# Four smallest experts last, summed in one tile, and a final layernorm that starts beside them

## The chip, the cores and the metric

The kernel runs on one core of a Trainium2 chip. The metric is the device time of one execution in microseconds (us); lower is better. A core has TensorE (PE, matrix products into PSUM), VectorE (DVE), ScalarE (ACT), GpSimd (POOL) and SyncE (SP, which here only issues transfers). Each engine works through its own instructions in program order and waits on semaphores of the others. Sixteen DMA engines serve the transfers that SyncE and GpSimd ask for.

## The reference, cut to what matters

One decoder layer over 1024 tokens of width 1024, all in float32: a token mixer, a first layernorm, and a mixture of 32 experts (512 hidden units), with a second layernorm at the end. The change touches only the mixture and the last layernorm.

```python
h2 = x * (1 + sc2) + sh2                       # the router and the experts read this
# top-1 of 4 groups, then top-2 of that group's 8 experts: 2 experts for each token
gu = h2[tokens_of_e] @ w_up[e]                 # 1024 x 1024
m[tokens_of_e] += weight * ((silu(gu[:, :512]) * gu[:, 512:]) @ w_down[e])   # 512 x 1024
x = _layernorm(ALPHA * x + (1 + g2) * m, ln2_g, ln2_b)       # over the 1024 columns
```

How many tokens an expert gets depends on the data; the mean is 64.

## The kernel before, in words

The mixer, the first layernorm and the routing take the first half of the time and aren't touched. They leave in DRAM `h2d` (the experts' inputs), `xad` (ALPHA times x, one row for each token, plus 128 spare rows for the padding of the lists) and `wd` (the weights of the tokens), and in SBUF the lists `tokp` and `aidp` (tokens of each expert) and `nhp` (a size code for each expert: over 9 means more than 32 tokens, over 11 more than 64, over 15 more than 128).

**Experts.** 32 experts are computed one after the other. The first four positions hold fixed experts; the other 28 are ordered by size (`places`, `reorder`): `place` gives the rank that stands at each position, so that large and small ones alternate. Positions 25 to 31 hold the ranks 28, 7, 29, 11, 30, 15, 31, where rank 31 is the smallest. Rank 7, at position 26, may have two blocks of 128 tokens.

**Weights.** Each expert has six tiles of 1 MB (four of w_up, two of w_down). SyncE asks for them in the order of `SEQ`: up(e), then down(e - 1). They go into 19 tiles of SBUF that are used in turn: `release` gives a tile back after its matmuls and asks for the next one (`eload`). After the last weights `late_v` reads the two layernorm vectors ln2_g and ln2_b into the two halves of a tile (`l2`), each repeated over 128 partitions.

**One step.** The step of expert e is: up(e) on the first two tiles, turn the hidden values of expert e - 1 (`turn_hidden`: four TensorE transposes, a ScalarE copy into `eh`), up(e) on the last two tiles, `hidden(e)` (Silu on ScalarE, product on VectorE), turn the tokens of e + 1, and `last_of(e - 1)`: `down`, then `finish`. GpSimd gathers the token rows and the weights ahead (`gather_first`, `gather_weight`). By `by_parts` a matmul takes the whole width for more than 64 tokens (`up_whole`, `down_whole`), and 64 or 32 columns of TensorE for fewer (`up_parts`, `down_parts`). `finish` multiplies the result by the weights on VectorE into `eyo` and adds it to the rows of `xad` by an accumulating indirect transfer from GpSimd (`scatter`). Each of these waits for the one before.

**Last layernorm.** After the experts all engines read a flag: if some expert has more blocks than were computed, a general loop does the rest (not taken with these inputs). Then SyncE reads the 1024 rows of `xad` as eight tiles `rt[0]` to `rt[7]` of 128 x 1024. `t_ops` gives the operations of a tile: mean and variance by VectorE (V in `TSTAT`) or by two ScalarE passes (S), a square root, and scaling and shifting divided among VectorE, GpSimd and ScalarE by `TMODE`. `TORDER` is the written-out order in which the operations of the eight tiles are issued. Each tile is then stored to `out`.

All instructions stand in program order on their engines (`manual_schedule`); nothing is moved by a scheduler.

Of the kernel before, what the change touches and what calls it, by code (L numbers as in the profile page):

```python
# [9 lines left out]
F32 = mybir.dt.float32  # L10
# [41 lines left out]
TSTAT = "VVVSVSVS"  # L52
TMODE = "pFBpFAFF"
TORDER = "00100102101213023231320425323423564546436567545653776777575"
# [5 lines left out]
def tile_hybrid_moe_layer(  # L60
# [786 lines left out]
    for j, (base, step) in enumerate(((16, 4), (FIXED, 1), (17, 4), (8, 1), (18, 4), (12, 1), (19, 4))):  # L847
        G.iota(spread[:, :, j], pattern=[[step, 4]], base=base, channel_multiplier=0, **imp)

# [442 lines left out]

    nmax = cst([P, 1], I32, "nmax")
    places()
# [94 lines left out]
    def down(e, ks, w):  # L1389
        p = pd(e)  # L1390

        def whole():
            down_whole(p, eh, ks, w)
            if e in TWO:
                with tc.If(N[e] > 15):
                    down_whole(pup2, eh2, ks, w)

        by_parts(N[e], whole, lambda m: down_parts(m, p, eh, ks, w))
# [87 lines left out]
    def last_of(e):  # L1486
        down(e, range(8, 12), weights_of(e, range(8, 12)))
        release(e, range(8, 12))
        finish(e)
        finish_second(e)  # L1490

    for e in range(NE):
        up(e, range(4), weights_of(e, range(4)))
# [30 lines left out]
    most = count(nmax, 0, None, 1)  # L1524
    with tc.If(most > 0):
# [30 lines left out]

    l2g, l2b = l2
    rt = [h for _ in range(4) for h in halves(unused.popleft())]
    for tt in range(8):
        nc.sync.dma_start(rt[tt], xad[tt * P:(tt + 1) * P, :])  # L1560
    st8 = p4.tile([P, 8, 2, 6], F32, name="st8")
    mv8 = p4.tile([P, 8, 2], F32, name="mv8")

    def t_ops(tt):
        r, mode = rt[tt], TMODE[tt]
        mu, sd = mv8[:, tt, 0:1], mv8[:, tt, 1:2]

        def moments():
            for n, sl in enumerate(COLS):
                V.bn_stats(st8[:, tt, n], r[:, sl])  # L1570

        def root(scale=1.0):
            S.activation(sd, sd, AF.Sqrt, bias=eps, scale=scale)

        def shift():
            if TSTAT[tt] == "V":
                V.scalar_tensor_tensor(mu, mu, -1.0, sd, op0=OP.mult, op1=OP.mult)
            else:
                V.tensor_tensor(mu, mu, sd, op=OP.mult)

        def part(q, sl, fused, e):
            v = (l2g, l2b)[q]
            if not fused:
                e.tensor_tensor(r[:, sl], r[:, sl], v[:, sl], op=(OP.mult, OP.add)[q])
            elif q:
                V.scalar_tensor_tensor(r[:, sl], r[:, sl], sd, v[:, sl], op0=OP.mult, op1=OP.add)
            else:
                V.scalar_tensor_tensor(r[:, sl], r[:, sl], mu, v[:, sl],
                                       op0=OP.subtract if TSTAT[tt] == "V" else OP.add, op1=OP.mult)

        def both(q):
            e = {"p": (G, G), "F": (V, V), "A": (G, V), "B": (V, G), "X": (V, V), "q": (G, G)}[mode][q]
            for sl in COLS if tt == 7 else [slice(0, D)]:
                part(q, sl, mode == "F", e)
                if q and tt == 7:
                    nc.sync.dma_start(out[0, tt * P:(tt + 1) * P, sl], r[:, sl])
            if q and tt < 7:
                nc.sync.dma_start(out[0, tt * P:(tt + 1) * P, :], r)

        if TSTAT[tt] == "V":  # L1600
            ops = [moments, lambda: V.bn_aggr(mv8[:, tt], st8[:, tt]), root]
        else:
            ops = [lambda: S.activation(eyo[0], r, AF.Copy, accum_out=mu),
                   lambda: V.tensor_scalar(mu, mu, -1.0 / D, None, op0=OP.mult),
                   lambda: S.activation(eyo[0], r, AF.Square, bias=mu, accum_out=sd),
                   lambda: root(1.0 / D)]
        ops.append(lambda: V.reciprocal(sd, sd))
        if mode == "q":
            ops.append(lambda: V.tensor_scalar(r, r, mu, sd, op0=OP.subtract if TSTAT[tt] == "V" else OP.add,
                                               op1=OP.mult))  # L1610
        elif mode != "F":
            ops += [shift, lambda: S.activation(r, r, AF.Identity, bias=mu, scale=sd)]
        return ops + [lambda: both(0), lambda: both(1)]

    t_all = [t_ops(tt) for tt in range(8)]
    for tt in TORDER:
        run(t_all[int(tt)], 1)
# [23 lines left out]
```

## Time and profile before

| | us |
|---|---|
| median of 3 runs (lowest to highest) | 1169.26 (1168.99 to 1174.07) |
| the profiled execution, its own time | 1171.18 |
| its span | 1169.3 |
| TensorE busy in the span | 1038.5 (89%) |
| VectorE busy | 553.8 (47%) |
| ScalarE busy | 292.7 (25%) |
| GpSimd busy | 358.9 (31%) |

The span is the stretch from the first to the last instruction that the profiler saw; times below are us from its start. The granted clock is the share of its full 2.4 GHz at which TensorE ran; it has two levels, 1.00 (2.4 GHz) and 0.50 (1.2 GHz), and a mean of a stretch can lie between. DMA share is the mean busy share of the sixteen DMA engines. Over the whole span 304.50 MB were moved.

### The profile page before, as it was taken

Reading aid. Unit: us, or ns where it says so; the run is one execution under the profiler, and the core shown is the slowest. Engines: PE = TensorE matmul, PEld = TensorE weight load, DVE = VectorE, ACT = ScalarE, POOL = GpSimd, SP = SyncE. Lnnn points to the kernel's source line nnn. Section 1 sums busy time; section 2 is a strip of 40 time slices with the busy share of each in tenths; the row PEclk is TensorE's granted clock in tenths of the full one; section 3 lists DMA queues with packets and bytes.
Section 4 is the critical chain, followed back from the end, with each engine's and each line's share of the span. In section 5 each row is a group of like instructions: output and inputs, shape, how many; then the busy total and the mean of one; then the engine's idle time right before and its main releaser. Section 6 shows DMA issues by size and latency. Waiting matters only on the chain.

```text
span 1169.3 us, 16712 instructions
## 1 busy us (share of the span) xinstructions
PE 1038.5 (89%) x5758; PEld 687.5 (59%) x5758; DVE 553.8 (47%) x1018; ACT 292.7 (25%) x440; POOL 358.9 (31%) x271
## 2 busy tenths in 40 slices
PE   4999999899999989998678999899999999899920
PEld 3778888788788767777433454454444544454510
DVE  6858975737664489999511211130223113211338
ACT  3363326643224442221210110010011101110113
POOL 2325543262211236543412211231134113301225
PEclk9899999999999999999798999999999999899975
DMA  9954454444212325414999989999999999999964
GB/s 277 247 168 145 131 182 140 142 144 144 91 51 59 144 88 221 164 68 187 371 361 345 393 338 323 381 394 412 386 377 380 412 389 373 390 416 394 387 222 179
DMA packets 93631, 304.50 MB, mean 260 GB/s; under 512 B 14769, under 2 KB 42073, under 8 KB 68909
## 3 DMA queue, kind: packets, MB, share of 16 engines
q1 hardware_dynamic: 83900, 275.52, 63.4%
q0 software_dynamic: 8368, 22.90, 7.3%
q10 hardware_dynamic: 1216, 4.21, 0.9%
q8 instruction: 83, 1.36, 0.5%
q14 instruction: 64, 0.52, 0.1%
HBM read 281.09 MB, written 22.88 MB: 260 GB/s over the span
## 4 chain that ended last, share of the span: by engine, by line
PE 27%; DMA 25%; issue 25%; DVE 16%; ACT 3%; POOLq 1%; POOL 1%; SPq 1%; DVEq 0%; ACTq 0%
DMA xad<-yo,tokp 19%; DMA wr<-wd,aidp 4%; PE sm L302 4%; PE acc L623 3%; PE acc L625 3%; PE acc L624 3%; PE acc L621 2%; PE acc L619 2%; PE acc L620 2%; DVE y1a L234 1%; DMA wd<-w 1%; DVE pc L1022 1%; DVE Fg L886 1%; DMA xad<-Vv 1%; SPq L103 1%
## 5 line engine op out<-in xcount | busy, mean ns | idle before, releaser
L1406 DVE TENSOR_TENSOR act<-up,act 128x512 f32<-128x512 f32 x32 | 22.1, 692 | 299.7 <-ACT act L1405 244.3
L1427 POOL DMA_INDIRECT xad<-yo,tokp x36 | 52.9, 1470 | 231.7 <-DVE yo L1423 106.1
L1423 DVE SCALAR_TENSOR_TENSOR yo<-dn,wr,g2p 32x256 f32<-32x256 f32 (+2 forms) x94 | 52.1, 563 | 126.9 <-PE ov L1359 39.0
L1412 ACT ACTIVATE eh<-tp 128x512 f32<-128x512 f32 x36 | 21.1, 596 | 315.5 <-PE tp L1411 274.8
L623 PE MATMUL acc<-whi,hTh 128*128 128x512 f32 x192 | 83.1, 433 | 0.0
L1212 POOL DMA_INDIRECT KS<-h2d,tokp x32 | 30.6, 958 | 164.0 <-PE tp L1319 155.1
L166 ACT ACTIVATE whi<-wr 128x1024 fp32r<-128x1024 f32 (+1 forms) x44 | 44.9, 1021 | 128.1 <-PE acc L625 67.9
L625 PE MATMUL acc<-whi,hTl 128*128 128x512 f32 x192 | 76.0, 396 | 0.0
L624 PE MATMUL acc<-wlo,hTh 128*128 128x512 f32 x192 | 75.4, 393 | 0.0
L167 POOL TENSOR_TENSOR wlo<-wr,whi 128x1024 fp32r<-128x1024 f32 (+1 forms) x15 | 35.8, 2385 | 119.9 <-ACT whi L166 108.3
L302 PEld LDWEIGHTS sm<-QP,KS 128*128 128x128 f32 x448 | 58.2, 192 | 7.3 <-issue 3.3
L619 PE MATMUL acc<-hTh,whi 128*128 128x512 f32 x144 | 59.3, 411 | 0.0
L302 PE MATMUL sm<-QP,KS 128*128 128x64 f32 x448 | 56.1, 269 | 2.6 <-DVE KS L315 1.6
L1344 PE MATMUL up<-pring,ext 128*128 128x512 f32 x128 | 56.7, 593 | 1.6 <-DVE yo L1423 1.6
L621 PE MATMUL acc<-hTh,wlo 128*128 128x512 f32 x144 | 56.9, 395 | 0.5 <-DVE wlo L167 0.3
L881 PE MATMUL pa<-wh,yl 128*128 128x512 f32 (+1 forms) x128 | 51.8, 405 | 5.5 <-DVE yl L865 5.5
L620 PE MATMUL acc<-hTl,whi 128*128 128x512 f32 x144 | 56.7, 393 | 0.0
L880 PE MATMUL pa<-wl,yh 128*128 128x512 f32 (+1 forms) x128 | 51.3, 401 | 4.7 <-DVE wl L1052 4.7
L879 PE MATMUL pa<-wh,yh 128*128 128x512 f32 (+1 forms) x128 | 53.4, 417 | 1.5 <-ACT wh L1051 0.9
L1405 ACT ACTIVATE act<-up 128x512 f32<-128x512 f32 x32 | 19.1, 597 | 135.2 <-PE ov L1344 52.3
L443 POOL TENSOR_TENSOR vec<-vec,y1a 128x1024 f32<-128x1024 f32 x14 | 35.4, 2527 | 55.2 <-ACT y1a L442 55.2
L167 DVE TENSOR_TENSOR wlo<-wr,whi 128x1024 fp32r<-128x1024 f32 (+1 forms) x29 | 38.4, 1324 | 22.6 <-ACT whi L166 21.9
(476 smaller groups left out, 2243.2 us busy)
## 6 DMA issues: line engine op xcount, KB each, us to landing
pring<-in_w_up SPq DMA_DIRECT2D x52, 1024.0 KB, 20.5
pring<-in_w_down SPq DMA_DIRECT2D x28, 1024.0 KB, 8.5
ring<-in_w_up SPq DMA_DIRECT2D x28, 1024.0 KB, 16.4
wr<-in_w_in SPq DMA_DIRECT2D x44, 512.0 KB, 6.0
y1a<-in_w_ada SPq DMA_DIRECT2D x32, 512.0 KB, 4.0
ring<-in_w_down SPq DMA_DIRECT2D x12, 1024.0 KB, 20.4
y0a<-in_w_up SPq DMA_DIRECT2D x8, 1024.0 KB, 15.1
y0b<-in_w_up SPq DMA_DIRECT2D x8, 1024.0 KB, 24.3
```

The source lines that it names most:

```text
L167: (G if u % 3 == 2 and u > W8 else V).tensor_tensor(lo, w, hi, op=OP.subtract)
L302: PE.matmul(p[:, hd], chd(KS)[:, c4, hd], chd(QP)[:, c4, hd].rearrange("p (b two i) -> p b two i", two=2, i=h)[:, :, 1, :], start=True, st ...
L619: PE.matmul(a[i], hi[:, j, sl], hTh[k], start=st, stop=False)
L620: PE.matmul(a[i], hi[:, j, sl], hTl[k], start=False, stop=False)
L621: PE.matmul(a[i], lo[:, j, sl], hTh[k], start=False, stop=sp)
L623: PE.matmul(a[i], hTh[k][:, sl], hi[:, j], start=st, stop=False)
L624: PE.matmul(a[i], hTh[k][:, sl], lo[:, j], start=False, stop=False)
L625: PE.matmul(a[i], hTl[k][:, sl], hi[:, j], start=False, stop=sp)
L879: PE.matmul(p, yh[:, k], wh[k][:, sl], start=k == 0, stop=False)
L1344: PE.matmul(p[:, h], x[:, k], gate_up(w[k], 2, h), start=k == 0, stop=k == 7)
L1423: V.scalar_tensor_tensor(yo[rows, n * c:(n + 1) * c], src, w[rows], g2p[rows, n * c:(n + 1) * c], op0=OP.mult, op1=OP.mult)
L1427: G.indirect_dma_start(out=xad, out_offset=bass.IndirectOffsetOnAxis(ap=tcol[rows], axis=0), in_=yo[rows], in_offset=None, bounds_check=T ...
```

## The change

- **Order of experts.** Positions 25 and 27 now hold the ranks 15 and 11, and positions 28 to 31 the ranks 28 to 31: the four smallest come last.
- **Their results.** If none of the four has more than 32 tokens and no general loop is needed (flag `slow` is 0), their results aren't scattered: `finish` writes each into 32 rows of one tile `yo2`. One 128 x 128 matrix `same_` (1 where two rows belong to the same token) sums the rows of one token on TensorE (`late_sum`). The rows of `xad` of these tokens are gathered into `base`, the sum is added, the result normalized (`late_stats`, `late_norm`) and written over the plain result by an indirect store (`late_store`).
- **All rows.** At the end of step 29, after the last weights and the two vectors have been asked for, SyncE asks for all eight tiles of `xad` (`late_start`); they hold everything but the last four experts.
- **Normalization.** Its operations are issued in eight groups, `norms(0)` to `norms(7)`, some within steps 31 and after it. GpSimd has no share in them. Tiles 0, 2 and 4 (P) are scaled and shifted on TensorE by a diagonal matrix and a product of ones with ln2_b, and taken out of PSUM by ScalarE; the others take two VectorE passes. Statistics are VectorE's for tiles 0 and 3 and ScalarE's for the others.
- **The last expert's** hidden values are turned into `eh2`, as `eh` takes the diagonals.
- If `slow` isn't 0, the four are scattered as before, the rows are read again and normalized after that.

```diff
-TSTAT = "VVVSVSVS"
-TMODE = "pFBpFAFF"
-TORDER = "00100102101213023231320425323423564546436567545653776777575"
+TSTAT = "VSSVSSSS"
+TMODE = "PFPFPFFF"
+TORDER = "001012001X02132X2451106X71X022X22XX23435647334535464654574576664777".split("X")
+LATE0 = 28
...
+    for o, n, base in ((25, 1, 15), (27, 1, 11), (LATE0, 4, LATE0)):
+        G.iota(place[:, o:o + n], pattern=[[1, n]], base=base, channel_multiplier=0, **imp)
...
+        V.tensor_reduce(slowi, nhp[:, LATE0:NE], axis=AX.X, op=OP.max)
+        V.tensor_scalar(slowi, slowi, 9.0, None, op0=OP.is_gt)
+        V.tensor_tensor(slowi, slowi, nmax, op=OP.max)
+        for i in range(4):
+            V.tensor_copy(tokl[32 * i:32 * (i + 1)], tokp[0:32, 0, LATE0 + i:LATE0 + i + 1])
+        V.tensor_copy(tokf, tokl)
...
     def finish(e):
+        if e < LATE0:
+            finish_any(e)
+            return
+        r = 32 * (e - LATE0)
+        with tc.If(slow[0] > 0) as large:
+            finish_any(e)
+        with large.Else():
+            for q in range(4):
+                sl = slice(q * 256, (q + 1) * 256)
+                V.scalar_tensor_tensor(yo2[r:r + 32, sl], pd(e)[32 * q:32 * (q + 1), 0, 0:256], wr[e % 2][0:32],
+                                       g2p[0:32, sl], op0=OP.mult, op1=OP.mult)
+
+    slow = []
+
+    def finish_any(e):
         yo = eyo[e % 2]
...
-    def last_of(e):
-        down(e, range(8, 12), weights_of(e, range(8, 12)))
+    def last_of(e, between=lambda: None, h=eh):
+        down(e, range(8, 12), weights_of(e, range(8, 12)), h)
         release(e, range(8, 12))
+        between()
         finish(e)
         finish_second(e)
...
+    base = xg[2]
...
+    def late_loads():
+        for tt in range(8):
+            nc.sync.dma_start(rt[tt], xad[tt * P:(tt + 1) * P, :])
+
+    def late_start():
+        rt.extend(h for _ in range(4) for h in halves(unused.popleft()))
+        late_loads()
+        G.indirect_dma_start(out=base, out_offset=None, in_=xad,
+                             in_offset=bass.IndirectOffsetOnAxis(ap=tokl, axis=0), bounds_check=T + P - 1,
+                             oob_is_err=False)
+        V.tensor_scalar(act2[:, 0:P], ones, tokf, None, op0=OP.mult)
+        p = tp()
+        PE.matmul(p[:, 0], act2[:, 0:P], ident, start=True, stop=True)
+        V.tensor_scalar(same_, p[:, 0], tokf, None, op0=OP.is_equal)
+
+    def late_sum():
+        for n in range(2):
+            PE.matmul(pup2[:, n], same_, yo2[:, COLS[n]], start=True, stop=True)
+
+    mu8, sd8 = mv8[:, 8, 0:1], mv8[:, 8, 1:2]
+
+    def late_stats():
+        for n, sl in enumerate(COLS):
+            V.tensor_tensor(base[:, sl], pup2[:, n], base[:, sl], op=OP.add)
+            V.bn_stats(st8[:, 8, n], base[:, sl])
+        V.bn_aggr(mv8[:, 8], st8[:, 8])
+        S.activation(sd8, sd8, AF.Sqrt, bias=eps)
+
+    def late_norm():
+        V.reciprocal(sd8, sd8)
+        V.scalar_tensor_tensor(base, base, mu8, l2[0], op0=OP.subtract, op1=OP.mult)
+        V.scalar_tensor_tensor(base, base, sd8, l2[1], op0=OP.mult, op1=OP.add)
+
+    def late_store():
+        G.indirect_dma_start(out=out[0], out_offset=bass.IndirectOffsetOnAxis(ap=tokl, axis=0), in_=base,
+                             in_offset=None, bounds_check=T - 1, oob_is_err=False)
+
+    def t_ops(tt):
...
+        def centre(sl):
+            V.scalar_tensor_tensor(r[:, sl], r[:, sl], mu, l2[0][:, sl],
+                                   op0=OP.subtract if TSTAT[tt] == "V" else OP.add, op1=OP.mult)
...
+        dg, pt = eh[:, tt % 4], (pup, pdn)[TMODE[:tt].count("P") % 2]
+
+        def scaled():
+            for n, sl in enumerate(COLS):
+                PE.matmul(pt[:, n], ones[0:1], l2[1][0:1, sl], start=True, stop=False)
+                PE.matmul(pt[:, n], dg, r[:, sl], start=False, stop=True)
+
+        def evict():
+            for n, sl in enumerate(COLS):
+                S.activation(r[:, sl], pt[:, n], AF.Copy)
+            store(slice(0, D))
+
+        def finished():
+            for sl in COLS if tt == 7 else [slice(0, D)]:
+                V.scalar_tensor_tensor(r[:, sl], r[:, sl], sd, l2[1][:, sl], op0=OP.mult, op1=OP.add)
+                store(sl)
+
+        if TSTAT[tt] == "V":
+            ops = [moments, lambda: V.bn_aggr(mv8[:, tt], st8[:, tt]), root]
+        else:
+            ops = [lambda: S.activation(junk[0], r, AF.Copy, accum_out=mu),
+                   lambda: V.tensor_scalar(mu, mu, -1.0 / D, None, op0=OP.mult),
+                   lambda: S.activation(junk[0], r, AF.Square, bias=mu, accum_out=sd),
+                   lambda: root(1.0 / D)]
+        ops += [lambda: V.reciprocal(sd, sd), lambda: centre(slice(0, D))]
+        if mode == "P":
+            return ops + [lambda: S.activation(dg, ident, AF.Copy, scale=sd), scaled, evict]
+        return ops + [finished]
...
+    def norms(i):
...
+        for tt in TORDER[i]:
+            run(todo_norms[int(tt)], 1)
+
     for e in range(NE):
+        if e == LATE0:
+            slow.append(count(slowi, 0, [mybir.EngineType.DVE, mybir.EngineType.Pool], 1))
...
         up(e, range(4, 8), weights_of(e, range(4, 8)))
         release(e, range(4, 8))
+        if e == NE - 1:
+            norms(0)
         hidden(act, pup)
         hidden_second(e)
         turn_first(e + 1)
         if e:
-            last_of(e - 1)
+            last_of(e - 1, lambda: norms(1) if e == NE - 1 else None)
         if e + 1 < NE:
             turn_second(e + 1)
-    turn_hidden(act, eh)
-    turn_hidden_second(NE - 1)
-    last_of(NE - 1)
+        if e == LATE0 + 1:
+            late_start()
+        if e == NE - 2:
+            slow_all = count(slowi, 0, None, 1)
+    turn_hidden(act, eh2)
+    last_of(NE - 1, lambda: norms(2), eh2)
...
-    most = count(nmax, 0, None, 1)
-    with tc.If(most > 0):
+    with tc.If(slow_all > 0) as large:
...
+        late_loads()
+        rest_of = [t_ops(tt) for tt in range(8)]
+        for tt in "".join(TORDER):
+            run(rest_of[int(tt)], 1)
+    with large.Else():
+        norms(3)
+        late_sum()
+        norms(4)
+        late_stats()
+        norms(5)
+        norms(6)
+        late_norm()
+        norms(7)
+        late_store()
```

## Rows read from the trace of the kernel before

**Rows 1.** Busy time by stretches: engines' us, then granted clock, DMA share, GB/s.

```profile
1100.00:1112.00 12.00, 12.00 (x128) 6.17 (x128) 3.20 (x6) 2.39 (x4) 2.86 (x3) 1.00 1.01 368
1112.00:1124.00 12.00, 7.37 (x61) 2.81 (x52) 4.10 (x7) 2.48 (x3) 2.48 (x3) 1.00 0.67 233
1124.00:1133.00 9.00, 0.00 (x0) 0.00 (x0) 0.00 (x0) 0.00 (x0) 1.31 (x1) 0.50 0.24 65
...
1008.00:1015.00 7.00, 5.72 (x46) 3.10 (x49) 1.38 (x2) 1.19 (x2) 0.99 (x1) 0.52 1.01 407
```

**Rows 2.** Timeline of SyncE's queue, 1098 to 1166: start, us, line, transfer.

```profile
1098.17 0.33 SPq L103 DMA_DIRECT2D gs<-in_w_down  x1
...
1102.76 0.34 SPq L1458 DMA_DIRECT2D vn<-in_ln_b  x1
...
1130.58 0.81 SPq L1560 DMA_DIRECT2D y0a<-xad  x2
...
1133.46 0.88 SPq L1560 DMA_DIRECT2D uu<-xad  x2
...
1165.42 0.33 SPq L1598 DMA_DIRECT2D out<-y1a  x1
```

**Rows 3.** DMA issues from 1090 on: count, size, median us to landing.

```profile
uu<-xad SPq DMA_DIRECT2D x2, 512.0 KB, 10.1
...
vn<-in_ln_b SPq DMA_DIRECT2D x1, 512.0 KB, 20.6
...
xad<-yo,tokp POOLq DMA_INDIRECT x5, 5.9
```

**Rows 4.** Timeline of TensorE, matmuls: start, us, output, array and shape, count.

```profile
1045.93 1.07 PE L1366 MATMUL dn<-uu,eh 128*32 128x256 f32 x16
...
1082.74 1.07 PE L1366 MATMUL dn<-ring,eh 128*32 128x256 f32 x16
...
1090.10 3.60 PE L1359 MATMUL dn<-y1a,eh 128*128 128x512 f32 x8
...
1106.06 1.93 PE L1366 MATMUL dn<-pring,eh 128*32 128x256 f32 x32
...
1115.63 1.94 PE L1366 MATMUL dn<-ring,eh 128*64 128x512 f32 x8 [0.22 <-DMA ring<-in_w_down]
...
1120.78 1.07 PE L1366 MATMUL ov<-gs,eh 128*32 128x256 f32 x16 [0.72 <-DMA gs<-in_w_down]
```

**Rows 5.** What SyncE's queue waited for from 1090 on.

```profile
SPq L1560 <- DMA xad<-yo,tokp: 21.5, 1, 21.5
...
SPq L1637 <- DMA out<-y1a: 1.6, 1, 1.6
```

**Rows 6.** Timeline of GpSimd: two scatters and what they waited for.

```profile
1080.73 1.44 POOL L1427 DMA_INDIRECT xad<-yo,tokp  x1 [9.47 <-DMA xad<-yo,tokp]
...
1125.52 1.31 POOL L1427 DMA_INDIRECT xad<-yo,tokp  x1 [4.64 <-issue]
```

**Rows 7.** Timeline of ScalarE, 1112 to 1160.

```profile
1112.52 0.60 ACT L1405 ACTIVATE act<-up 128x512 f32<-128x512 f32 x1 [1.32 <-PE up L1354]
...
1121.49 1.28 ACT L1573 ACT_TABLE_LOAD   x1 [2.56 <-ACTq L1525]
...
1139.03 1.06 ACT L1603 ACTIVATE yo<-y0b 128x1024 f32<-128x1024 f32 x1 [0.48 <-DMA y0b<-xad]
...
1158.31 1.15 ACT L1605 ACTIVATE yo<-uu,mv 128x1024 f32<-128x1024 f32 x1
```

**Rows 8.** Timeline of VectorE, 1113 to 1158.

```profile
1113.15 0.69 DVE L1406 TENSOR_TENSOR act<-up,act 128x512 f32<-128x512 f32 x1 [3.10 <-ACT act L1405]
...
1133.88 1.29 DVE L1570 BATCH_NORM_STATS2 st<-y0a 128x6 f32<-128x512 f32 x2 [10.01 <-DMA y0a<-xad]
...
1142.05 0.14 DVE L1607 RECIPROCAL mv<-mv 128x1 f32<-128x1 f32 x1
1142.12 3.23 DVE L1586 SCALAR_TENSOR_TENSOR y0a<-y0a,mv,vn 128x1024 f32<-128x1024 f32 x1
...
1156.94 1.27 DVE L1588 SCALAR_TENSOR_TENSOR uu<-uu,mv,vn 128x1024 f32<-128x1024 f32 x1
```

More of the change, by code (lines that the diff above doesn't have):

```diff
@@ L1291, in reorder @@
         V.tensor_reduce(nmax, nb, axis=AX.X, op=OP.max)
+        V.tensor_reduce(slowi, nhp[:, LATE0:NE], axis=AX.X, op=OP.max)
[4 more added lines that the diff above has]
+        V.tensor_copy(tokf, tokl)
     nmax = cst([P, 1], I32, "nmax")
+    slowi = p4.tile([P, 1], I32, name="slow")
+    tokl = p4.tile([P, 1], I32, name="tokl")
+    tokf = p4.tile([P, 1], F32, name="tokf")
     places()
@@ L1387, in up, with down @@
         by_parts(N[e], whole, lambda m: up_parts(m, pup, ext[b], ks, w))
-    def down(e, ks, w):
+    def down(e, ks, w, h):
         p = pd(e)
         def whole():
-            down_whole(p, eh, ks, w)
+            down_whole(p, h, ks, w)
             if e in TWO:
@@ L1396, in whole @@
                     down_whole(pup2, eh2, ks, w)
-        by_parts(N[e], whole, lambda m: down_parts(m, p, eh, ks, w))
+        by_parts(N[e], whole, lambda m: down_parts(m, p, h, ks, w))
     def pd(e):
@@ L1484, in tile_hybrid_moe_layer @@
     turn_second(0)
-    def last_of(e):
-        down(e, range(8, 12), weights_of(e, range(8, 12)))
+    def last_of(e, between=lambda: None, h=eh):
+        down(e, range(8, 12), weights_of(e, range(8, 12)), h)
         release(e, range(8, 12))
+        between()
         finish(e)
         finish_second(e)
+    st8 = p4.tile([P, 9, 2, 6], F32, name="st8")
+    mv8 = p4.tile([P, 9, 2], F32, name="mv8")
+    rt, junk = [], []
+    base = xg[2]
+    same_ = p4.tile([P, P], F32, name="same")
+    def late_loads():
+        for tt in range(8):
+            nc.sync.dma_start(rt[tt], xad[tt * P:(tt + 1) * P, :])
@@ new lines, in late_store, with moments, root, store @@
+    def late_store():
+        G.indirect_dma_start(out=out[0], out_offset=bass.IndirectOffsetOnAxis(ap=tokl, axis=0), in_=base,
+                             in_offset=None, bounds_check=T - 1, oob_is_err=False)
+    def t_ops(tt):
+        r, mode = rt[tt], TMODE[tt]
+        mu, sd = mv8[:, tt, 0:1], mv8[:, tt, 1:2]
+        def moments():
+            for n, sl in enumerate(COLS):
+                V.bn_stats(st8[:, tt, n], r[:, sl])
+        def root(scale=1.0):
+            S.activation(sd, sd, AF.Sqrt, bias=eps, scale=scale)
+        def centre(sl):
+            V.scalar_tensor_tensor(r[:, sl], r[:, sl], mu, l2[0][:, sl],
+                                   op0=OP.subtract if TSTAT[tt] == "V" else OP.add, op1=OP.mult)
+        def store(sl):
+            nc.sync.dma_start(out[0, tt * P:(tt + 1) * P, sl], r[:, sl])
+        dg, pt = eh[:, tt % 4], (pup, pdn)[TMODE[:tt].count("P") % 2]
[4 more added lines that the diff above has]
+        def evict():
+            for n, sl in enumerate(COLS):
+                S.activation(r[:, sl], pt[:, n], AF.Copy)
[15 more added lines that the diff above has]
+        return ops + [finished]
@@ L1492, in tile_hybrid_moe_layer @@
+    todo_norms = []
+    def norms(i):
+        if not todo_norms:
+            junk.append(eyo[0])
+            todo_norms.extend(t_ops(tt) for tt in range(8))
+        for tt in TORDER[i]:
+            run(todo_norms[int(tt)], 1)
     for e in range(NE):
+        if e == LATE0:
+            slow.append(count(slowi, 0, [mybir.EngineType.DVE, mybir.EngineType.Pool], 1))
         up(e, range(4), weights_of(e, range(4)))
@@ L1554, in tile_hybrid_moe_layer @@
                     scatter(eyo[0], icol[:, 0:1], slice(0, P))
[L1557 to L1613, printed above, removed]
@@ L1615, in tile_hybrid_moe_layer @@
-    t_all = [t_ops(tt) for tt in range(8)]
-    for tt in TORDER:
-        run(t_all[int(tt)], 1)
+        late_loads()
[12 more added lines that the diff above has]
+        late_store()
 _INS = ['x', 'c', 'w_ada', 'b_ada', 'w_in', 'lb_logits', 'hg_norm_w', 'sg_ln_g', 'sg_ln_b', 'sg_w', 'sg_b',
```

## The prediction

> **What bounds the kernel now.** I read the stretches of the end first [rows 1]. Up to 1112 the DMA engines are busy all the time at about 370 GB/s and TensorE works without a gap: the expert stage is held by the stream of weights, with TensorE close behind it. From 1112 to 1124 TensorE has work for 7.4 of 12 us, then none at all, and its granted clock goes from 1.00 (2.4 GHz) to 0.50 (1.2 GHz). SyncE's queue says when things were asked for [rows 2]: the last weights (gs) at 1098.17, the second layernorm vector (ln_b) at 1102.76. The landings say what that means [rows 3]: ln_b took 20.6 us although it is half a megabyte, so it landed at 1123.4, behind the seven to eight megabytes that 20.6 us hold at that rate. TensorE shows the same [rows 4]: expert 30's second down tile was waited for until 1115.6, expert 31's last until 1120.8.
>
> So the tail begins at 1121.9 and has three pieces: the scatter of expert 31 and SyncE's wait for it (21.5 us by the row, of which 8.7 lie after TensorE's end) until the rows are asked for at 1130.58 [rows 2, 5, 6]; the eight rows landing from 1133.9 on, rt[3] at 1139.0, so 1.4 to 1.7 us apart, the last issue 10.1 us after it was asked [rows 3, 7, 8]; and normalization until the last store at 1165.42, whose landing is waited for 1.6 us, with the span ending 1.9 us later [rows 2, 5]. That is 47 us.
>
> **What is removed and moved.** The four scatters of experts 28 to 31 go, and with them the wait that held the row loads. GpSimd's share of the normalization goes; it had stretched VectorE's 1024-wide pass from 1.27 to 3.23 us [rows 8], so a pass now counts 1.27. The four smallest do take the short path: in the kernel before they stand at positions 25, 27, 29 and 31, and all four show matmuls 32 columns wide, so at most 32 tokens [rows 4]. The larger experts move ahead: a down projection of 16 instructions at 0.43 (8 take 3.44, start to start) instead of 1.93 us at position 27, some 1.7 more at 25, and 10 us more of up projection that position 28 then lacks. Expert 27's down would end near 1093, its scatter go out near 1102 behind those of 26, each of which waits some 9 us for the one before [rows 6], and land near 1112. That is still inside the weight stream, so it costs nothing; weights are asked for up to 7 us later around position 28, out of over 20 us that they lie in the queue. If that cover were gone, each microsecond would move the last weights by one.
>
> **Where the rows now land.** They are asked for behind ln_b in SyncE's program, on the same queue. The row of ln_b therefore sets them: rt[0] at 1123.4 + 1.4 = 1124.8, rt[1] 1126.2, rt[2] 1127.6, rt[7] 1134.6. The bound below is a queue whose sixteen engines end together: the 67% DMA share of 1112 to 1124 [rows 1] would give back 4 us, rt[0] at 1120.8. I take 1124.8, since ln_b measured exactly this place in the queue.
>
> **What then waits.** The operations called norms(0) stand ahead of hidden(31) on ScalarE and VectorE, which work in program order. ScalarE must copy rt[1] and rt[2] and square rt[1] before it may take the Silu of the last expert, which was ready at 1112.5 [rows 7]. And Sqrt and Silu each need their table: the row has one load of 1.28, the change needs three. From 1126.2: copy 1.25 (1.06 and the accumulator's read), load 1.28, root 0.3, copy 1.25, square 1.35, load 1.28, Silu 0.6: 7.3, so 1133.5. The Trainium skill (ScalarE: Activation LUTs, What ACT_TABLE_LOAD costs) speaks against the change here: it gives about 2.66 us for a switch of sets, drain included, where this row has 1.28; by it the sum would end about 4 us later, by the row as given.
>
> VectorE's product 0.7 [rows 8], TensorE's turn of four transposes, and on ScalarE the diagonal, a third load, a root and a square (3.2) before it may copy eh2 (0.6): 1137.5. Expert 31's down is 2.05 us at full clock [rows 4]; TensorE has by then been idle for some 17 us, and idle gaps brought its clock to 0.5 in both stretches shown [rows 1]; so 4.1, end 1141.6. Before, it ended at 1121.85.
>
> **The rest of the chain.** scaled() of tile 0 is queued on TensorE ahead of late_sum: 8 instructions of 0.43 are 3.45 at full clock, 6.9 at half; I take 5.2, as the clock may come back in it: 1146.9. late_sum, 4 instructions: 1.75, and a branch and gaps 0.6: 1149.2. late_stats: twice (0.69 + 0.65) and 0.2, then a root of 0.3: 1152.7 with its gaps. Next, ScalarE stands in a queue: the diagonal of tile 2 (0.3), scaled() of tile 2 (5.5), two evictions (1.2), and only then the root of tile 3: 1160.2. VectorE has by then done late_norm and waits. It still has nine passes of 1.27, five reciprocals of 0.15 and some 0.7 of gaps: 1172.9. The last stores leave by 1173.5 and land by 1175.6. late_store writes rows that these stores also write, so it must wait for them: 1.4 to issue [rows 6] and 3.0 to land, then the 1.9 to the span's end: 1181.9. For that landing the bounds are 2.0 (a plain store) and 5.9 (the median scatter here [rows 3]); I take 3.0, being a plain write through GpSimd's queue. The base gather and the last two weight gathers on GpSimd come near 1112 to 1121, hidden behind the wait for the rows.
>
> The span goes from 1169.3 to 1181.9, so 12.6 more. The profiled execution's own time is 1171.18, 1.9 over its span and 1.9 over the median of the runs; laid on the median 1169.26 this is 1182 us, 1.1% slower.
>
> **Rivals.**
> *Rows late, chain short (C).* The queue ends together (rt[0] at 1120.8) and TensorE keeps 2.4 GHz: minus 4 for the rows, and minus 6 for the down, scaled() and evictions together. 1172. For it: DMA share falls before the weights end; against it: the clock rows. Within 0.5%.
>
> *Rows early (B), on the other side.* If the rows land by 1110, ahead of the end of the weights, hidden(31) isn't held, the last down waits for its weights alone (1120.8), and TensorE has no long gap, so it keeps its clock as it did to 1124 [rows 1]. The chain then starts some 15 us earlier and runs 6 shorter: 1161, 0.7% faster. It decides where rt[2] lands: every microsecond there is one at the end, and with the clock at full the point of no change is rt[0] near 1118. Against it stands the row of ln_b; for it, only that a third of the engines' time is free from 1112 on.
>
> *Weights late (D).* The release of slots, later by up to 7 us around position 28, leaves the queue short, or the short path isn't taken and scatters, rows and normalization come in turn. Each microsecond adds one; 1188 for a loss of 6. Against it: the depth of the queue.
>
> **How the numbers follow.** The forecast (A: rows behind the weights, gate held, clock partly low) has 0.60, with 1176 to 1190 as its own range: both ends of the clock (minus 6, plus 6), the landing (minus 1, plus 3), the rows (minus 4). C has 0.18, B 0.14, D 0.08. Timing of this kernel can tell 0.5% from no change, 5.8 us. So faster 0.14, same 0.18, slower 0.68. The range leaves out B and the far end of A and D: 1166 to 1190.
>
> **What would show it.** In the changed profile: the first two Copy operations of ScalarE on rows after 1124, the Silu of expert 31 near 1133 with a table load in front of it, three table loads after 1110, the last down near 1138 to 1142, a granted clock of 0.5 there, VectorE idle near 1150 and near 1156 to 1160, and a GpSimd indirect store that waits for the last plain store. Wrong would be: rows that land before 1115, the last weights before 1115 or after 1126, a scaled() of 3.5 us, or a late_store that doesn't wait.

## The result and the profile after

The changed kernel takes 1184.18 us (median of 4 runs, 1183.02 to 1188.02) against 1169.90 for the kernel before on the same chip: a ratio of 1.0117, 95% interval 1.0101 to 1.0132. It is slower, as forecast. Its profiled span is 1181.5 us, 12.2 over that of before. "Before" and "earlier" compare moments in two profiles, each counted from the start of its own span.

SyncE's queue in the timeline of the changed kernel (start, us, line, transfer), against [rows 2]:

```profile
1097.22 0.33 SPq L104 DMA_DIRECT2D gs<-in_w_down  x1
...
1103.18 0.34 SPq L1486 DMA_DIRECT2D vn<-in_ln_b  x1
...
1115.77 0.80 SPq L1532 DMA_DIRECT2D y0a<-xad  x2
...
1123.33 1.61 SPq L1532 DMA_DIRECT2D uu<-xad  x2
```

The DMA issues from 1090 us on (count, size, median us to landing), against [rows 3]:

```profile
vn<-in_ln_b SPq DMA_DIRECT2D x1, 512.0 KB, 21.4
...
out<-wsg,tokl POOLq DMA_INDIRECT x1, 3.2
```

What SyncE's queue waited for, against [rows 5]:

```profile
SPq L1532 <- DMA xad<-yo,tokp: 12.1, 1, 12.1
```

The rows are asked for 14.8 us earlier than before (1115.77 for 1130.58), since the wait for scatters is 12.1 us and no longer 21.5. But ln_b, asked at 1103.18, took 21.4 us and landed at 1124.6, and the rows stand behind it. Their first use shows what of the 14.8 us arrives.

The timeline of the changed kernel, all engines, without the weight loads (in brackets: idle before, and what ended it; the idle time of the first row's use is put down to the row load that ended last by the profile, here y1a):

```profile
1104.45 1.95 DVE L1454 SCALAR_TENSOR_TENSOR yo<-dn,wr,g2p 32x256 f32<-32x256 f32 x4 [4.25 <-DMA wr<-wd,aidp]
...
1106.76 0.77 PE L1542 MATMUL tp<-ident,act 128*128 128x128 f32 x2 [5.55 <-DVE act L1540]
...
1125.98 1.29 DVE L1573 BATCH_NORM_STATS2 st<-y0a 128x6 f32<-128x512 f32 x2 [7.17 <-DMA y1a<-xad]
1127.22 1.06 ACT L1606 ACTIVATE yo<-y0a 128x1024 f32<-128x1024 f32 x1 [7.25 <-DMA y0a<-xad]
...
1128.39 1.28 ACT L1576 ACT_TABLE_LOAD   x1
...
1132.31 1.28 ACT L1418 ACT_TABLE_LOAD   x1
1133.60 0.60 ACT L1418 ACTIVATE act<-up 128x512 f32<-128x512 f32 x1
...
1134.51 1.28 ACT L1576 ACT_TABLE_LOAD   x1
...
1139.47 1.93 PE L1379 MATMUL ov<-gs,eh 128*32 128x256 f32 x16
...
1145.78 1.88 PE L1547 MATMUL ov<-yo,same 128*128 128x512 f32 x4
...
1154.48 2.08 PE L1591 MATMUL dn<-y0b,eh 128*128 128x512 f32 x2
...
1156.59 1.08 ACT L1595 ACTIVATE y0b<-dn 128x512 f32<-128x512 f32 x2 [5.30 <-PE dn L1591]
...
1157.89 0.16 DVE L1610 RECIPROCAL mv<-mv 128x1 f32<-128x1 f32 x1 [3.87 <-ACT mv L1576]
...
1168.26 1.41 DVE L1600 SCALAR_TENSOR_TENSOR uu<-uu,mv,vn 128x512 f32<-128x512 f32 x2
...
1174.95 1.02 POOL L1564 DMA_INDIRECT out<-wsg,tokl  x1 [54.87 <-POOLq L1663]
```

The first row is used at 1125.98, only 7.9 us earlier than before (1133.88). The Silu of expert 31 runs at 1133.60 behind two row copies, a root, a square and two table loads; before it ran at 1112.52. The last down ends at 1141.40, 19.6 us later than before. VectorE waits 3.87 us for the root of tile 3, which stands on ScalarE behind evictions that wait for scaled() of tile 2. VectorE ends at 1169.67, and the second write of the late rows starts at 1174.95.

The same end by stretches (columns as in [rows 1]):

```profile
1112.00:1124.00 12.00, 11.16 (x172) 6.41 (x164) 3.21 (x6) 2.30 (x4) 2.99 (x3) 1.00 0.97 362
1124.00:1136.00 12.00, 1.02 (x4) 0.73 (x4) 4.78 (x10) 8.66 (x13) 0.00 (x0) 0.68 0.62 244
1136.00:1140.00 4.00, 2.35 (x25) 1.09 (x28) 3.45 (x7) 3.65 (x8) 0.00 (x0) 0.50 0.00 0
1140.00:1144.00 4.00, 4.00 (x21) 1.33 (x14) 1.93 (x4) 2.31 (x5) 0.00 (x0) 0.75 0.06 14
1144.00:1148.00 4.00, 4.00 (x9) 1.40 (x9) 2.85 (x4) 1.62 (x4) 0.00 (x0) 1.00 0.36 141
...
1152.00:1160.00 8.00, 6.56 (x8) 1.50 (x6) 4.06 (x10) 3.37 (x7) 0.00 (x0) 0.52 0.16 66
1160.00:1170.00 10.00, 6.08 (x6) 1.50 (x6) 9.57 (x13) 4.97 (x12) 0.00 (x0) 0.50 0.39 158
```

The DMA engines are full until 1124 (share 0.97), where before a third of their time was free from 1112 on. TensorE is idle for 11 of the 12 us from 1124 on and comes back at a granted clock of 0.50 (1.2 GHz).

### The profile page after: what moved, and what is told of

Read it like the earlier page. It is cut to its first block, busy times and chain, and to the rows that moved or that the text cites. A ratio compares the mean times of both kernels' runs of the same rounds, so it can differ in the third digit from the quotient of the medians.

```text
span 1181.5 us, 16784 instructions
## 1 busy us (share of the span) xinstructions
PE 1065.1 (90%) x5788; PEld 695.1 (59%) x5788; DVE 550.6 (47%) x1028; ACT 301.7 (26%) x460; POOL 339.0 (29%) x266
## 5 line engine op out<-in xcount | busy, mean ns | idle before, releaser
L1440 POOL DMA_INDIRECT xad<-yo,tokp x32 | 47.5, 1486 | 210.0 <-DVE yo L1436 97.0
L1436 DVE SCALAR_TENSOR_TENSOR yo<-dn,wr,g2p 32x256 f32<-32x256 f32 (+2 forms) x82 | 46.4, 576 | 122.3 <-PE ov L1372 38.8
L625 PE MATMUL acc<-wlo,hTh 128*128 128x512 f32 x192 | 75.2, 392 | 0.0
L1357 PE MATMUL up<-pring,ext 128*128 128x512 f32 x152 | 67.2, 594 | 1.6 <-DVE yo L1436 1.6
L1357 PEld LDWEIGHTS up<-pring,ext 128*128 128x128 f32 x152 | 28.3, 191 | 35.7 <-issue 34.9
```

Source lines behind the costliest of these rows:

```text
L625: PE.matmul(a[i], hTh[k][:, sl], lo[:, j], start=False, stop=False)
L1357: PE.matmul(p[:, h], x[:, k], gate_up(w[k], 2, h), start=k == 0, stop=k == 7)
L1440: G.indirect_dma_start(out=xad, out_offset=bass.IndirectOffsetOnAxis(ap=tcol[rows], axis=0), in_=yo[rows], in_offset=None, bounds_check=T ...
```

## The experiments

All runs but one alter the changed kernel. Up to the last expert's weights all of these but the two with short tiles do the same work, and yet the last weights (gs) were asked for anywhere from 1093.69 to 1099.35. A difference of 2 to 5 us between two profiles can thus lie ahead of the tail. So beside the median there is T, the profiled span less the time at which gs was asked for. The kernel before has T = 1169.3 - 1098.17 = 71.1, the changed one 84.3.

T stands on one profile of each run, and the tail varies too. The run without the second write does the same work as the changed kernel up to VectorE's last step, and yet that step ends 75.2 us after gs was asked for (1172.65 - 1097.47) instead of 72.5 (1169.67 - 1097.22). Two ratios are clear of each other, by their intervals, only from about 0.23% (2.7 us) on. So by either measure a difference of less than some 3 us is not shown.

| run | median us | ratio to before, 95% | gs asked | T |
|---|---|---|---|---|
| changed | 1184.18 | 1.0117 [1.0101, 1.0132] | 1097.22 | 84.3 |
| normalization behind the last expert | 1177.64 | 1.0064 [1.0047, 1.0081] | 1094.92 | 79.6 |
| filler products | 1181.99 | 1.0100 [1.0080, 1.0120] | 1096.52 | 83.6 |
| before, with the new order | 1175.34 | 1.0045 [1.0029, 1.0062] | 1095.70 | 77.6 |
| no second write | 1177.14 | 1.0066 [1.0047, 1.0085] | 1097.47 | 80.4 |
| rows on GpSimd's queue | 1184.77 | 1.0125 [1.0105, 1.0145] | 1096.71 | 86.6 |
| short tiles | 1180.16 | 1.0095 [1.0079, 1.0112] | 1094.35 | 82.3 |
| other steps, in the branch | 1180.51 | 1.0094 [1.0077, 1.0111] | 1096.59 | 82.4 |
| all tiles by VectorE | 1180.41 | 1.0095 [1.0078, 1.0112] | 1095.05 | 83.8 |
| the same, short tiles | 1171.73 | 1.0014 [0.9997, 1.0031] | 1094.75 | 75.5 |
| interleaved anew, two tiles by TensorE | 1170.06 | 0.9996 [0.9979, 1.0012] | 1099.35 | 71.3 |
| interleaved anew, all by VectorE | 1169.19 | 0.9990 [0.9974, 1.0005] | 1093.69 | 71.7 |

### Normalization behind the last expert

```diff
-        if e == NE - 1:
-            norms(0)
...
-            last_of(e - 1, lambda: norms(1) if e == NE - 1 else None)
+            last_of(e - 1)
...
-    last_of(NE - 1, lambda: norms(2), eh2)
+    last_of(NE - 1, h=eh2)
+    for i in range(3):
+        norms(i)
```

> The changed kernel (median 1184.2 us, span 1181.5) with one move: norms(0), norms(1) and norms(2) are issued after the last expert's down projection and finish instead of ahead of and between them. Theory (the rows land behind the weights and hold the last expert): the Silu of expert 31 comes at about 1121.5 instead of 1133.6, its down ends near 1125.5 instead of 1141.4, one table load less lies on ScalarE's path; the rows then have ScalarE and VectorE alone from 1126 on, and the end comes 5 to 7 us earlier (about 1178). Rival 1 (the tail is bound by the sum of VectorE's and ScalarE's work after the rows land, whatever the order): less than 2 us. Rival 2 (the late sum then waits longer behind scaled() of tile 0, and nothing is won): 0.

Measured: 6.5 us less by the medians, 4.7 by T: within the theory by the medians, a little under it by T. (The steps ahead of hidden(31) that hold the last expert are called the gate below, and this run the run without the gate.) Its timeline:

```profile
1100.69 0.34 SPq L1486 DMA_DIRECT2D vn<-in_ln_b  x1
...
1119.17 0.60 ACT L1418 ACTIVATE act<-up 128x512 f32<-128x512 f32 x1 [1.32 <-PE up L1367]
...
1126.19 1.28 ACT L1576 ACT_TABLE_LOAD   x1
...
1150.92 0.16 DVE L1610 RECIPROCAL mv<-mv 128x1 f32<-128x1 f32 x1 [4.74 <-ACT mv L1576]
```

The Silu now waits for TensorE alone, and comes 18.5 us after ln_b was asked for instead of 30.4. One table load is left of three. So the steps ahead of hidden(31) held the last expert by 12 us, of which 4.7 to 6.5 reach the end. The rest goes into the wait for the root of tile 3, which grew from 3.87 to 4.74, and, it seems, into other gaps: VectorE is busy for only 6.23 and 5.19 of 10 us in the two stretches from 1134 to 1154 of this run:

```profile
1134.00:1144.00 10.00, 7.36 (x11) 2.64 (x10) 6.23 (x10) 4.64 (x10) 0.00 (x0) 0.67 0.28 110
1144.00:1154.00 10.00, 7.59 (x8) 1.50 (x7) 5.19 (x12) 4.31 (x10) 0.00 (x0) 0.50 0.13 52
```

### Filler products that keep TensorE's clock up

```diff
+    def fill(n):
+        p = tp().rearrange("p a b -> p (a b)")
+        for _ in range(n):
+            PE.matmul(p[:, 0:256], ones, g2p[:, 0:256], start=True, stop=True)
...
         def scaled():
+            fill({2: 7, 4: 12}.get(tt, 0))
...
-            last_of(e - 1, lambda: norms(1) if e == NE - 1 else None)
+            last_of(e - 1, lambda: (norms(1), fill(24)) if e == NE - 1 else None)
```

> The changed kernel with 43 extra TensorE products of ones with g2p (128 x 256, results unused) in TensorE's idle stretches: 24 behind down(30), 7 ahead of scaled() of tile 2, 12 ahead of that of tile 4. Theory (TensorE's lower clock lengthens the chain through the last down, scaled() and the late sum): the granted clock stays near 1.0 from 1124 to 1165, the last down takes 2 instead of 3.7 us, scaled() of tile 2 from its diagonal on 2.6 to 3.5 instead of 5.2 us, and the end comes 3 to 5 us earlier (about 1180). Rival (scaled() and the evictions are hidden behind VectorE's passes): less than 1 us.

Measured: 2.2 us less by the medians, 0.7 by T, neither clear of the changed kernel. Three of its windows, and its evictions of tile 2:

```profile
1124.00:1136.00 12.00, 9.52 (x46) 8.06 (x45) 3.98 (x9) 7.88 (x12) 0.00 (x0) 1.00 0.55 216
1136.00:1152.00 16.00, 13.96 (x61) 6.93 (x61) 11.20 (x19) 8.35 (x16) 0.00 (x0) 0.79 0.18 71
1152.00:1160.00 8.00, 8.00 (x27) 4.50 (x27) 5.33 (x13) 3.88 (x9) 0.00 (x0) 1.00 0.16 66
```

```profile
1156.67 1.09 ACT L1601 ACTIVATE y0b<-dn 128x512 f32<-128x512 f32 x2 [3.63 <-PE dn L1597]
```

The clock did rise: 1.00 over 1124 to 1136 (0.68 in the changed kernel), and 1.00 over 1152 to 1160 (0.52). Between them, where the last down, the products of tile 0 and late_sum run, it was 0.79. The evictions of tile 2 still came at 1156.67 (1156.59 in the changed kernel), as the fillers stand on TensorE ahead of the products that they speed up. The theory's 3 to 5 us aren't there. What the low clock costs by itself stays open.

### The kernel before with the new order of experts alone

```diff
+    for o, n, base in ((25, 1, 15), (27, 1, 11), (28, 4, 28)):
+        G.iota(place[:, o:o + n], pattern=[[1, n]], base=base, channel_multiplier=0, **imp)
```

> The kernel before (1169.3) with the new order of experts alone: ranks 15 and 11 at positions 25 and 27, ranks 28 to 31 last; all four are still scattered and the old tail follows. Theory: the weights end at the same time, but the scatters of 26 (two), 27, 28, 29, 30 and 31 wait for each other, the one of 27 only goes out near 1104, each of the rest takes 5 to 11 us, so the rows are asked for near 1137 to 1142 instead of 1130.6: 5 to 12 us slower than before. Rival (the order is free, as the weights set the end): within 2 us of before.

Measured: 1175.34, 5.5 us over before, 6.5 by T, at the low end of the theory. Scatters in its timeline of GpSimd:

```profile
1102.81 1.62 POOL L1429 DMA_INDIRECT xad<-yo,tokp  x1 [4.82 <-DMA xad<-yo,tokp]
1114.81 1.36 POOL L1429 DMA_INDIRECT xad<-yo,tokp  x1 [9.03 <-DMA xad<-yo,tokp]
```

The first is expert 27's, which waits 4.82 us for the second of expert 26's to land; the second is expert 28's, which waits 9.03 us for expert 27's. In this kernel four in all stand behind expert 27's, and the rows are asked for at 1134.68 instead of 1130.58 (39.0 us after gs instead of 32.4). The changed kernel has no scatters behind it, but its rows wait for the same one (12.1 us above).

GpSimd's queue is late there too. The gather of expert 28's weights goes out at 1097.04, behind the second scatter of expert 26 (1095.30), and VectorE waits 4.25 us for it until 1104.45. The product that late_start gives TensorE waits for VectorE behind that, so TensorE stood idle for 5.55 us at 1101 to 1107. How much of this wait is the order's isn't shown; the run with the order alone has no such product.

### Without the second write

```diff
         norms(7)
-        late_store()
```

> The changed kernel without late_store: the rows of the last four experts are computed but not written over the plain ones, so those rows lack the last four experts' share. Theory (late_store waits for the last plain store to land and then adds its own issue and landing): the end comes 4.5 to 6 us earlier, about 1179. Rival (its landing is covered by the kernel's end): less than 2 us.

This run leaves out the write of the late rows. Measured: 7.0 us less by the medians, a little over the theory, and 3.9 by T; in its profile the evictions of tile 2 came 3.0 later than in the changed kernel's. TensorE's clock was 0.73 over 1140 to 1144 and 0.69 over 1144 to 1148 there (0.75 and 1.00 in the changed kernel), and the products of tile 0 and late_sum took 7.8 us instead of 6.3. VectorE's last step:

```profile
1171.23 1.42 DVE L1600 SCALAR_TENSOR_TENSOR uu<-uu,mv,vn 128x512 f32<-128x512 f32 x2
```

From VectorE's last step to the end of the span it has 1177.9 - 1172.65 = 5.3 us, where the changed kernel has 1181.5 - 1169.67 = 11.8: the write costs 6.6.

### The rows on GpSimd's queue

```diff
-    def late_loads():
+    def late_loads(q=nc.sync):
         for tt in range(8):
-            nc.sync.dma_start(rt[tt], xad[tt * P:(tt + 1) * P, :])
+            q.dma_start(rt[tt], xad[tt * P:(tt + 1) * P, :])
...
-        late_loads()
+        late_loads(G)
```

> The changed kernel (median 1184.2 us, span 1181.5) with one change: the eight row tiles are asked for on GpSimd's queue, ahead of the base gather, instead of on SyncE's behind the weights. They still wait for the scatter of expert 27 (1115.7). Theory (in SyncE's queue the rows stand behind the weights): on a queue of their own they share the engines with the last weights; rt[0] lands near 1119 to 1121 instead of 1126, rt[2] near 1123, the Silu of expert 31 comes 4 to 6 us earlier and so does the end (about 1178 to 1180); the last weights land 2 to 3 us later, which nobody waits for. Rival (a row tile takes some 10 us from being asked for whatever the queue, as the engines are full): less than 1.5 us.

Measured: 1184.77, no gain. The theory's 4 to 6 us failed, and the rival has the time right but not its reason, as the rows did come earlier past the queue (first used 25.9 us after gs was asked for instead of 28.8), and the last down ended 1.7 us earlier counted from gs (1139.2 - 1096.71 against 1141.40 - 1097.22). It was lost behind that. Timeline and windows of this run:

```profile
1122.57 1.29 DVE L1573 BATCH_NORM_STATS2 st<-y0a 128x6 f32<-128x512 f32 x2 [4.30 <-DMA y0a<-xad]
...
1131.39 0.60 ACT L1418 ACTIVATE act<-up 128x512 f32<-128x512 f32 x1
...
1145.13 2.08 PE L1591 MATMUL up<-y0a,eh 128*128 128x512 f32 x2
```

```profile
1136.00:1148.00 12.00, 12.00 (x42) 3.99 (x35) 6.10 (x10) 5.36 (x10) 0.00 (x0) 0.50 0.13 50
```

TensorE stays at 0.50 over 1136 to 1148, so the four product rows of tile 0 take 8.1 us (1139.12 to 1147.21) instead of 4.6 (1141.33 to 1145.94), and late_sum stands behind them. Why the clock stayed low in this run isn't shown; in the run without the second write, with the steps as in the changed kernel, the same products took 5.0.

### Short tiles for the last expert, with and without TensorE

Two runs read 16 of 2048 columns of expert 31's weight tiles, so that the rows' place in the queue comes earlier; the last expert's result is stale data there. One alters the changed kernel, the other the run "all tiles by VectorE", which comes first.

```diff
-TMODE = "PFPFPFFF"
-TORDER = "001012001X02132X2451106X71X022X22XX23435647334535464654574576664777".split("X")
+TMODE = "FFFFFFFF"
+TORDER = "001012001X2132X245116X71X022XXX234356473345354646557576664777".split("X")
```

> The changed kernel with tiles 0, 2 and 4 scaled and shifted by VectorE like the others (two passes of 1.27 us) instead of over TensorE and ScalarE; the order of all other operations is kept. Theory (scaled() holds ScalarE's queue at the evictions, so that VectorE waits some 4 us for the root of tile 3; what the route spares VectorE it loses there): within 2 us of the changed kernel. Rival (the route over TensorE spares VectorE three passes): 3 to 4 us slower.

Measured: 3.8 us less by the medians, 2.6 by the ratios and 0.5 by T, so not clear of the changed kernel: whether the route through TensorE costs something in this order stays open. The rival's 3 to 4 us more for leaving it didn't come.

```diff
-            load(RAW[i], w_at(*SEQ[i]))
+            if SEQ[i][0] == NE - 1:
+                load(RAW[i][:, 0:16], w_at(*SEQ[i])[:, 0:16])
+            else:
+                load(RAW[i], w_at(*SEQ[i]))
```

> The changed kernel with expert 31's six weight tiles read only in their first 16 columns (of 2048), the rest of the tiles being stale: its result isn't the model's, all else is as it was. About 6 MB less stand ahead of the rows in SyncE's queue; the rows are then asked for when the scatter of expert 27 has landed (1114 to 1116). Theory (each microsecond that the rows land earlier takes one off the end): rt[0] near 1119 to 1120 instead of 1126, the end 5 to 7 us earlier (about 1178), although TensorE's and VectorE's work is the same. Rival (the chain behind the last down sets the end, not the rows): the end moves by less than 2 us.

> The run in which VectorE finishes every tile, with the last expert's weights read 16 columns wide as in the run with the short tiles (its result is stale data). Theory: without the products on TensorE, rows that stand 10 us earlier are worth nearly all of it: 7 to 9 us below the run in which VectorE finishes every tile, 1171 to 1174. Rival (the late tile's product and the last expert hold the tail whichever engine finishes the tiles): 3 to 4.5 us below it, 1176 to 1177.5, as the short tiles gave in the changed kernel.

Timeline of the first (with TensorE), then of the second:

```profile
1107.11 1.58 SPq L1535 DMA_DIRECT2D y0a<-xad  x2
...
1122.93 0.60 ACT L1421 ACTIVATE act<-up 128x512 f32<-128x512 f32 x1
...
1138.53 3.62 PE L1550 MATMUL ov<-yo,same 128*128 128x512 f32 x4
...
1170.07 1.02 POOL L1567 DMA_INDIRECT out<-wsg,tokl  x1 [53.28 <-POOLq L1666]
```

```profile
1107.70 1.28 SPq L1535 DMA_DIRECT2D y0a<-xad  x2
...
1123.00 0.60 ACT L1421 ACTIVATE act<-up 128x512 f32<-128x512 f32 x1
...
1132.69 3.75 PE L1550 MATMUL ov<-yo,same 128*128 128x512 f32 x4 [2.19 <-DVE yo L1457]
...
1163.66 1.02 POOL L1567 DMA_INDIRECT out<-wsg,tokl  x1 [47.00 <-POOLq L1666]
```

In both the Silu comes some 8 us earlier from gs (28.6 and 28.2 us after it, against 36.4 and 36.6). With TensorE, 2.0 of 7.8 us remain at the end by T (4.0 by the medians); there late_sum stands behind tile 0's products at half clock, and ends 11.4 us after the last down instead of 6.3. Without it, all 8.3 remain (8.7 by the medians). The theory for the second run held, the 5 to 7 us for the first failed. So in these two orders rows that come earlier are worth one for one where no product of a tile stands between the last down and late_sum, and less where one does; how much less is known only to some 3 us.

### The steps interleaved anew

First with everything in the branch:

```diff
-TSTAT = "VSSVSSSS"
-TMODE = "PFPFPFFF"
+TSTAT = "VSSSSSSS"
+TMODE = "FFPPPFFF"
...
```

> The changed kernel with hidden(31), the last down and both finishes ahead of all normalization, and with another order of it, all behind the flag: tile 0 has VectorE's statistics and the others ScalarE's, tiles 2, 3 and 4 go over TensorE, and each operation is put where its engine is free (late_sum after three operations, late_stats after eighteen more, late_norm at the end). Theory (rows from 1124 on, one table load, no engine waiting behind another's late operation): VectorE is busy nearly all the time from 1125 on and done near 1156 instead of 1169.7; the span is 1162 to 1168, against 1169.3 before the change and 1174.5 with the gate alone removed: the first version that is at or under the kernel before (0 to 0.6% faster). Rival (the late store's tail and the rows' landing keep it from falling under the kernel before): 1170 or more.

Here (TORDER, not shown, is new as well) norms(0) to norms(2) are taken out of the last expert and all steps stand in the branch; the product of tile 4 overwrites that of tile 2 before it is taken out, so the output is another. Measured: 1180.51, T 82.4; the theory failed. The first row is used at 1131.90 there, 35.3 us after gs was asked for (28.8 in the changed kernel). The three tiles on TensorE ran one behind the other:

```profile
1141.00:1147.00 6.00, 6.00 (x7) 1.49 (x7) 5.93 (x10) 5.93 (x13) 0.00 (x0) 0.50 0.26 104
1147.00:1155.00 8.00, 8.00 (x9) 1.98 (x9) 7.91 (x11) 2.16 (x7) 0.00 (x0) 0.50 0.14 54
1155.00:1163.00 8.00, 7.98 (x8) 1.89 (x8) 1.36 (x2) 1.08 (x2) 0.00 (x0) 0.50 0.33 131
```

VectorE is through by 1157, and TensorE, at 0.50 all the time, works on alone.

Then behind the last expert but ahead of the branch, once with two tiles on TensorE and once with none (of the first only the core is shown; the second has TSTAT "SSSVSSSS", TMODE "FFFFFFFF" and a TORDER of its own):

```diff
-TSTAT = "VSSVSSSS"
-TMODE = "PFPFPFFF"
+TSTAT = "VSSSSSSS"
+TMODE = "FPFFPFFF"
+TORDER = "01X234001132140633X161513174305550467375547544662147277466222".split("X")
...
-    last_of(NE - 1, lambda: norms(2), eh2)
+    last_of(NE - 1, h=eh2)
+    norms(0)
+    late_sum()
+    norms(1)
+    late_stats()
+    norms(2)
+    late_norm()
```

> The changed kernel with the normalization behind the last expert and ahead of the branch (only the second write of the late rows stays in it), tile 0's sums by VectorE and the other seven by ScalarE, tiles 1 and 4 through TensorE, and the steps of all tiles interleaved anew. What it changes: the branch for inputs that need more rows than the fixed ones would come too late for it; for these inputs nothing is left out. Theory (the last expert is held by what is issued ahead of it, 6.5 us; the rest is the order of steps and TensorE's products at their slow 2.0 us): Silu(31) at about 1119, the last VectorE step at 1157 to 1161 where the changed kernel has 1169.7, span 1165 to 1170, time 1168 to 1173. Rival (the products through TensorE hold ScalarE's queue whatever the order, some 4 us): span 1171 to 1175, slower than its sister without them.

> As the sister run, but no tile goes through TensorE: tile 3's sums by VectorE, the other seven by ScalarE, every multiplication by VectorE, interleaved anew. What it changes: the same as there. Theory: VectorE is the bound from the rows' landing on: eight tiles of two passes of 2.6 to 2.8 us, the late tile's six passes of about 1.4 us and its statistics, some 55 us of work between 1116 and the end with gaps of some us while the last expert's evictions run, so its last step at 1159 to 1163, span 1167 to 1172, time 1170 to 1175. Rival (VectorE's passes wait for ScalarE's sums as in the changed kernel): span 1174 to 1177.

Measured: 1170.06, within the theory's 1168 to 1173, and 1169.19, 0.8 below the range of the other; VectorE's last step ended at 1159.74 and 1157.27. T is 71.3 and 71.7: the 13 us that the change cost are gone, with the order of experts, the row loads and the second write as in the changed kernel. Between the two, whose orders differ too, no gain or loss of the route through TensorE can be measured. Two windows of the first show why it is short:

```profile
1140.00:1150.00 10.00, 8.47 (x9) 2.46 (x10) 9.94 (x16) 9.84 (x22) 0.00 (x0) 0.50 0.37 149
1150.00:1158.00 8.00, 5.63 (x6) 1.04 (x5) 7.89 (x10) 2.15 (x5) 0.00 (x0) 0.50 0.44 170
```

VectorE has 17.8 of 18 us busy, where the run without the gate had 11.4 of 20 at the same stage. TensorE is at 0.50 here too; nobody waits for it. Neither version beats the kernel before by what can be measured; both are no slower. For inputs that need the general branch they aren't the same program, as it would come too late.

## Why the prediction was right

Forecast: 12.6 us more span, 1182 us, 1.1% slower. Measured: 12.2, 1184.18 and 1.2%. The main mechanism held (rows behind ln_b, the last expert held by the steps ahead of it, the second write at the very end); that the span agrees to 0.4 us is partly luck, as two errors of some 3 us cancel at the end.

- **The rows.** Forecast: rt[0] at 1124.8, behind ln_b. Measured: ln_b landed at 1124.6 and the first row was used 1.4 us later, 1125.98. The second was used 1.24 us after the first (1127.22), where 1.4 was forecast for their spacing. The start was 1.2 late: ln_b was asked for 0.4 later and took 0.8 longer.
- **The gate.** Forecast: 7.3 us from the copy of rt[1] to the end of the Silu, with two loads of 1.28. Measured: 1127.22 to 1134.20, 7.0. The run without the gate puts 4.7 to 6.5 us of the result on it. Each of the three loads starts within 0.02 us of the end of the operation before it, and the next one starts within 0.01 us behind it (1128.39 + 1.28, and the root at 1129.68). The Trainium skill (ScalarE: Activation LUTs, What ACT_TABLE_LOAD costs) gives the same 1.28 us for the load itself, but about 2.66 us for a switch with its drain. With that this trace does not agree: 1.28 is all that a switch took.
- **The last down.** Forecast 4.1 us, its end at 1141.6; measured 1137.76 to 1141.40, 3.6, at a granted clock of 0.50 up to 1140.
- **scaled() and late_sum.** Forecast 5.2 for tile 0, and late_sum's end at 1149.2. Measured 4.6 and 1147.66: the clock was back within tile 0 (0.75 over 1140 to 1144, 1.00 over 1144 to 1148).
- **The wait for the root of tile 3.** Forecast to end at 1160.2, measured 1157.86 (1157.56 + 0.30): the mechanism held, it was 2.3 too late, as late_sum had ended 1.5 earlier than forecast. VectorE's rest was 12.7 in the forecast and 11.8 in the trace, so its end was 1169.67 and not 1172.9.
- **The second write.** Forecast: 1.4 to issue and 3.0 to land, so 4.4. Measured 3.2 from its issue to its landing. Two other terms were too short: it was issued 5.3 us after VectorE's end (2.7 forecast), and the span ended 3.3 us after its landing (1.9 forecast). So the write took 2.8 longer than forecast, and VectorE had ended 3.2 earlier: 1181.5 against 1181.9, by luck and not by the terms.
- **What was wrong.** The new order was put down at nothing. By itself it sets the experts back: with the order alone the Silu of expert 31 comes 20.9 us after gs was asked for (1116.63 - 1095.70), where it was 14.4 before. In the changed kernel TensorE stands idle for 5.55 us behind late_start's product, which the forecast doesn't have either, and expert 31's up products ended at 1121.2, 24.0 us after gs. That cost nothing here only because the rows came later still. In the run without the gate the Silu comes 18.5 us after ln_b was asked for, where it was 9.8 before; what that costs there was not tried.
- **The rivals.** Weights late: refuted, gs was asked for at 1097.22, 1.0 earlier than before, and in the run without the gate nothing in expert 31's down waits for its weights. Rows late and a short chain: the rows did not come at 1120.8, which refutes it. Its 6 us for the clock weren't tried by the fillers, as they stood in the way themselves and the clock was 0.79 over 1136 to 1152. Rows early: it didn't happen. With short tiles the first row is used 7.6 us earlier counted from gs (1115.54 - 1094.35 against 1125.98 - 1097.22) and the Silu comes 7.8 earlier, but the changed kernel's own order gives only 2.0 of it at the end by T, 4.0 by the medians; the price of one for one was met only in the order without the route through TensorE.

## What to carry to other kernels

Before moving work ahead of a late dependency, look at what is queued behind it on each engine that works in program order: the gate cost 12 us on the last expert, and the normalization, issued behind it and interleaved so that VectorE hardly waits, cost 13 us less at the end than in the order of this change (with one tile less through TensorE, or none). Asking earlier on a queue that was still full gave less in arriving than in asking: 7.9 us for 14.8 (7.0 for 13.9 counted from gs). And a second write of the same rows stands behind the first, which put 6.6 us behind all other work here.

## What the runs showed of the hardware

In the run with all steps in the branch TensorE had 22.0 of 22 us busy from 1141 to 1163 and its granted clock stayed at 0.50 (1.2 GHz) throughout, each product of 512 columns taking 2.0 us start to start for its two instructions. In the changed kernel it was back at 1.00 in 1144 to 1148, with TensorE at work since 1137.76, and down again in 1152 to 1160, after a wait of 2.64 us. In the run without the second write TensorE was busy throughout 1140 to 1148 and the clock was 0.73 and then 0.69. These rows don't settle what brings the clock back.

The time up to the last weights differed by 5.7 us between profiles of kernels that are the same up to there (gs asked at 1093.69 to 1099.35). A comparison of tails must take that out. What is left is uncertain too: with the same work, VectorE's last step came 72.5 us after gs was asked for in one profile and 75.2 in another.
